# Last gathered rows moved into the last group's second half, gates loaded four keys at once and ahead, sums loaded later

## The chip, the cores and the metric

The kernel runs on one core of one Trainium2 chip. Its engines work beside each other, each through its own list of instructions in order: TensorE (PE, with PEld for its weight loads), VectorE (DVE), ScalarE (ACT), GpSimd (POOL) and SyncE (SP, which here only starts DMA transfers). The metric is the device time of one execution in microseconds (us). A time given for a kernel is the median of several executions; the profile comes from one more execution.

## The reference

One layer: a hybrid mixer, a cross attention over a memory, and a PEER feed-forward layer, each with a residual and a layer norm. The change touches the PEER layer alone. For each of 512 tokens, 8 heads pick 16 of 128 x 128 = 16,384 experts, so 128 experts a token:

```
def block(args):
    xt, it, gt = args
    u = expert_u[it]
    a = jnp.einsum('tkd,td->tk', u, xt, preferred_element_type=F32)
    hact = jax.nn.gelu(a, approximate=False) * gt
    return jnp.einsum('tk,tkd->td', hact.astype(x.dtype), expert_v[it])
...
h = peer_ffn(x, peer_wq[l], peer_sub_keys[l], peer_u[l], peer_v[l])
x = layer_norm(DN_ALPHA * x + h, ln_w[l, 2], ln_b[l, 2])
```

`it` holds the picked experts, `gt` their softmax gates. D is 2048, everything is float32.

## The kernel before, in words

The kernel does the PEER layer in two ways beside each other.

**Gathered half.** Tokens 0 to 255, in two blocks of 128 (`t` = 0 and 1). For each of the 128 picks `k` of a block, `job_u` gathers one row of `peer_u` per token (an indirect DMA of 128 rows of 8 KB, 1 MB, into a `rows` tile, line 1007) and DVE takes its dot product with the token (line 1027). When a block's 128 dots are there, `job_v` gathers rows of `peer_v` and DVE adds them, scaled, to the block's sum `x2l` (line 1043). After the last, `fin_gathered` makes the layer norm of the block and writes it out. `rows` has three buffers; they also serve the norm's weights (`lw`, line 1064) and, once all jobs are handed out and six further weight tiles were loaded, every second weight tile (`load_raw`).

**Dense half.** Tokens 256 to 511 (`H` = 256, two blocks of 128, `HB` = 2) go over all experts. There are `NC_` = 128 keys `c` of 128 experts each. A U tile (1 MB, `next_a`) gives the activations of one key: 48 matmuls into a PSUM bank `pa`, two keys to a bank; then ACT's gelu (line 1288) writes `ga`. 28 of the 64 pairs `ga` are spilled to DRAM (`gad`) and come back later as `gb`. Just ahead of the dense stage the gates are built as a full matrix and written to DRAM (`gd`, eight writes of 2 MB). `stage_h` loads the gates `G` of a pair of keys, multiplies them into `ga`, and splits the product into an upper and a lower part, `hph` and `hpl`. A V tile (1 MB) holds two keys and one half (`dh`) of the 2048 output columns: 24 matmuls into four banks `mm` (lines 1390, 1391 and 1399). Sixteen keys are a group (`J`), and `stage_o` runs a group's eight V tiles of the first column half, then eight of the second; then the banks are added to the sums `acc` (lines 1413 and 1415). 68 keys of U are done ahead of the first group; the rest are mixed into the V tiles by `fill` until they run out. After the last group comes the layer norm of both dense blocks (`fin`).

Each weight tile is split by ACT (upper part, line 179) and DVE (lower part, line 182) into one of two `ring` tiles; float32 is done as three products of such parts. In the dense stage there are three buffers for raw weight tiles.

**What sets the order.** A job is handed out by `tick`, which every split calls: it adds credit (`rate` x cost x `mult`; the rate is the number of jobs over 980 units), and for each whole credit the next gather is given to GpSimd, to start behind that split; its use on DVE is put behind the split two tiles later at the earliest (`lag`). A scheduler with a model of the times then lays each engine's instructions into one fixed order, in which a use can stand later still. The sync engine's list of loads is fixed in the same way; a load whose buffer is not free holds all loads behind it. `after(i, j)` keeps `i` behind `j` in that order without a wait on the chip. `ahead` is the table of how many U tiles are done by which key; `spilled` holds the pairs that go through `gad`.

Of the kernel before, what the change touches and what calls it, by code (L numbers as in the profile page):

```python
# [49 lines left out]
def build(tc, I, out):  # L50
    nc = tc.nc
    NC_ = PKEYS
    with ExitStack() as ctx:
# [981 lines left out]
        def job_v(t, k, s):  # L1035
            rows = gather("peer_v", t, k, s)

            def use(s2):
                d = tok[t]["dots"][k // GB]
                acc = tok[t]["x2l"]  # L1040
                if k == 0:
                    nc.vector.tensor_scalar(acc, acc, ALPHA, None, op0=ALU.mult)
                i = nc.vector.scalar_tensor_tensor(acc, rows, d[:, GB + k % GB:GB + k % GB + 1], acc,  # L1043
                                                   op0=ALU.mult, op1=ALU.add)
                after(i, s2)
                if k == NC_ - 1:
                    fin_gathered(t)
            return use
# [18 lines left out]
        def fin_gathered(t):  # L1067
            acc = tok[t]["x2l"]
            st = gat["pool"].tile([P, 32], F32, tag="fst", bufs=2, name=nm("fst"))
            fin_load()  # L1070
# [237 lines left out]
        def o_bank():  # L1308
            return mm_bank()
# [44 lines left out]
        hs = {}  # L1354
        state["mult"] = 1.0

        def stage_h(c):
            gt = mn.tile([P, H // 64, 2, 64], F32, tag="G", bufs=3, name=nm("G"))
            nc.sync.dma_start(gt, gd[:, :, c:c + 2])
            if c // 2 in spilled:  # L1360
                ga = mn.tile([P, 512], F32, tag="gb", bufs=3, name=nm("gb"))
                nc.sync.dma_start(ga, gad[c // 2])
            else:
                ga = gas.pop(c // 2)
# [8 lines left out]
        def stage_o(c0, dh, fill):  # L1373

            banks = [[o_bank() for g in range(2)] for t in range(HB)]
            for jj in range(J // 2):
                raw = load_raw(I["vD"][c0 // 2 + jj, dh])
                for vh, vl, o, w in shares(raw, 2.0):
                    for j in range(o // 1024, (o + w) // 1024):
# [3 lines left out]
                        if c0 == 0 and dh == 0 and c in (2, 4):  # L1383
                            nc.sync.dma_start(acc[c // 2 - 1], x2d[HB + c // 2 - 1].rearrange("p g c -> p (g c)"))
# [16 lines left out]
            last = c0 + J == NC_  # L1401
            if last and dh == 0:
                if state["done"] < len(jobs):
                    raise RuntimeError(f"{len(jobs) - state['done']} jobs left")
            if last and dh:
                while state["later"]:
                    state["later"].pop(0)[1](state["s"])
                fin_load()
# [24 lines left out]
        while at[0] < ahead[0]:  # L1433
            next_a()
# [88 lines left out]
```

## Time and profile before

| what | value |
|---|---|
| median of 3 runs | 4688.21 us (4683.93 to 4692.0) |
| the profiled execution's own time | 4692.06 us |
| its span | 4690.4 us |
| granted TensorE clock, mean | 0.983 |
| PE busy | 4466.1 us, 95% |
| DVE busy | 3764.6 us, 80% |
| ACT busy | 2233.0 us, 48% |
| POOL busy | 894.8 us, 19% |
| moved by DMA | 1490.81 MB, 318 GB/s over the span |

The page also cuts the span into 40 slices of 117 us; a digit is the busy share of a slice in tenths:

```profile
PE   8999999999999999999999988999989999999985
DVE  7877668557898877888788669799978998888886
PEclk9999999999999999999999999999999999999997
DMA  7899889666788889888799765667999999999995
GB/s 289 323 332 329 319 324 340 231 212 226 281 340 327 324 336 345 333 336 316 261 350 355 263 229 195 237 258 285 373 366 399 405 410 370 385 376 379 390 379 188
```

The dense stage with its V tiles lies in the last ten slices. A "wait" in the trace is time in which an engine stood still and what ended that; the chain of waits is followed back from the last instruction.

### The profile page before, as it was taken

How to read it: one execution, taken by the hardware profiler on the slowest of the kernel's cores; microseconds unless marked ns; L12 is line 12 of the kernel's file. 1: busy time of each engine (PE TensorE's matmuls, PEld its weight loads, DVE VectorE, ACT ScalarE, POOL GpSimd, SP SyncE). 2: the span in 40 equal slices, each digit the busy share in tenths (PEclk: the TensorE clock that was granted, in tenths of full speed). 3: DMA queues.
4: the chain of work that ended last, by engine and by line, in shares of the span. 5: the costliest groups of instructions: out<-in, count | busy, mean ns of one | idle time of the engine just before them, and what ended most of it. 6: DMA issues, size and time to landing. Idle time of an engine off the chain costs nothing. (4 is left out here: it accounts for less than half of the span.)

```text
span 4690.4 us, 65123 instructions
## 1 busy us (share of the span) xinstructions
PE 4466.1 (95%) x25662; PEld 3986.0 (85%) x25662; DVE 3764.6 (80%) x4234; ACT 2233.0 (48%) x3040; POOL 894.8 (19%) x631
## 2 busy tenths in 40 slices
PE   8999999999999999999999988999989999999985
PEld 6888888889888899999899766999988778889984
DVE  7877668557898877888788669799978998888886
ACT  6866766554344323333334674535744333343431
POOL 1000000000222222322221000112122333333430
PEclk9999999999999999999999999999999999999997
DMA  7899889666788889888799765667999999999995
GB/s 289 323 332 329 319 324 340 231 212 226 281 340 327 324 336 345 333 336 316 261 350 355 263 229 195 237 258 285 373 366 399 405 410 370 385 376 379 390 379 188
DMA packets 261204, 1490.81 MB, mean 318 GB/s; under 512 B 27132, under 2 KB 69180, under 8 KB 92320
## 3 DMA queue, kind: packets, MB, share of 16 engines
q1 hardware_dynamic: 167568, 890.57, 50.9%
q0 software_dynamic: 81664, 561.95, 31.0%
q10 hardware_dynamic: 11664, 34.12, 1.8%
q8 instruction: 201, 3.29, 0.3%
q14 instruction: 107, 0.88, 0.1%
HBM read 1427.24 MB, written 59.29 MB: 317 GB/s over the span
## 5 line engine op out<-in xcount | busy, mean ns | idle before, releaser
L179 ACT CAST ring<-raw 128x1024 fp32r<-128x1024 f32 x1568 | 1595.5, 1050 | 1585.5 <-PE mm L201 428.2
L182 DVE TENSOR_TENSOR ring<-raw,ring 128x2048 fp32r<-128x2048 f32 (+1 forms) x926 | 1810.2, 1961 | 574.3 <-ACT ring L179 306.9
L1007 POOL DMA_INDIRECT rows<-in_peer_u,ei x256 | 384.0, 1500 | 1676.6 <-DVE rows L1027 786.3
L201 PE MATMUL mm<-Ah,ring 128*128 128x384 f32 x2560 | 670.4, 342 | 13.4 <-ACT Ah L147 6.2
L1043 DVE SCALAR_TENSOR_TENSOR x2l<-rows,dots,x2l 128x2048 f32<-128x2048 f32 x256 | 601.0, 2348 | 49.5 <-DMA rows<-in_peer_v,ei 48.6
L1007 POOL DMA_INDIRECT rows<-in_peer_v,ei x256 | 443.9, 1734 | 929.3 <-DVE x2l L1043 696.6
L1027 DVE SCALAR_TENSOR_TENSOR rows<-rows,x2l 128x2048 f32<-128x2048 f32 x256 | 582.7, 2284 | 22.0 <-DMA rows<-in_peer_u,ei 21.8
L1277 PE MATMUL pa<-Xh,ring 128*128 128x256 f32 x2048 | 499.8, 285 | 32.3 <-ACT ring L179 16.8
L1280 PE MATMUL pa<-Xl,ring 128*128 128x256 f32 x2048 | 495.6, 282 | 0.0
L201 PEld LDWEIGHTS mm<-Ah,ring 128*128 128x128 f32 x2560 | 463.6, 189 | 20.6 <-ACT Ah L147 7.4
L1390 PE MATMUL mm<-ring,hph 128*128 128x512 f32 x1024 | 405.5, 396 | 63.0 <-ACT ring L179 62.6
L201 PE MATMUL mm<-Al,ring 128*128 128x384 f32 x1280 | 428.9, 341 | 0.6 <-DVE Al L148 0.6
L1277 PEld LDWEIGHTS pa<-Xh,ring 128*128 128x128 f32 x2048 | 389.3, 190 | 39.9 <-ACT ring L179 21.1
L1391 PE MATMUL mm<-ring,hpl 128*128 128x512 f32 x1024 | 403.4, 394 | 0.0
L1280 PEld LDWEIGHTS pa<-Xl,ring 128*128 128x128 f32 x2048 | 389.9, 190 | 2.9
L244 PE MATMUL mm<-ring,Zl 128*128 128x512 f32 x832 | 329.1, 396 | 0.0
L243 PE MATMUL mm<-ring,Zh 128*128 128x512 f32 x832 | 328.3, 395 | 0.7 <-ACT ring L179 0.7
L243 PE MATMUL mm<-ring,Ah 128*128 128x512 f32 x768 | 305.5, 398 | 1.1 <-ACT ring L179 1.1
L244 PE MATMUL mm<-ring,Al 128*128 128x512 f32 x768 | 303.4, 395 | 0.0
L1390 PEld LDWEIGHTS mm<-ring,hph 128*128 128x128 f32 x1024 | 193.9, 189 | 109.0 <-ACT ring L179 67.3
L1284 PE MATMUL pa<-Xh,ring 128*128 128x256 f32 x2048 | 265.7, 282 | 5.3 <-DVE ring L182 5.2
L201 PE MATMUL mm<-Bh,ring 128*128 128x384 f32 x1024 | 262.6, 339 | 5.6 <-ACT ring L179 4.9
(388 smaller groups left out, 7143.2 us busy)
## 6 DMA issues: line engine op xcount, KB each, us to landing
raw<-in_w_in SPq DMA_DIRECT2D x256, 1024.0 KB
raw<-in_uT SPq DMA_DIRECT2D x128, 1024.0 KB
raw<-in_vD SPq DMA_DIRECT2D x128, 1024.0 KB
raw<-in_w_out SPq DMA_DIRECT2D x48, 1024.0 KB
raw<-in_peer_wq SPq DMA_DIRECT2D x48, 1024.0 KB
raw<-in_w_xkv SPq DMA_DIRECT2D x32, 1024.0 KB
raw<-in_w_br_ml SPq DMA_DIRECT2D x32, 1024.0 KB
raw<-in_w_br_fx SPq DMA_DIRECT2D x32, 1024.0 KB
```

The source lines that it names most:

```text
L179: x = nc.scalar.copy(hi[:, c:c + 1024], src[:, c:c + 1024])
L182: s = nc.vector.tensor_sub(lo, src, hi.bitcast(F32))
L201: i = nc.tensor.matmul(o, w, x, start=start and s % per == 0, stop=stop and s % per == per - 1)
L243: nc.tensor.matmul(banks[t], xh[:, tt], wh[:, c], start=k == 0, stop=False)
L244: nc.tensor.matmul(banks[t], xl[:, tt], wh[:, c], start=False, stop=False)
L1007: i = nc.gpsimd.indirect_dma_start(out=rows, out_offset=None, in_=I[table], in_offset=bass.IndirectOffsetOnAxis(ap=ei[t][:, k:k + 1], axis=0))
L1027: i = nc.vector.scalar_tensor_tensor(rows, rows, 1.0, tok[t]["x2l"], op0=ALU.mult, op1=ALU.mult, accum_out=d[:, k % GB:k % GB + 1])
L1043: i = nc.vector.scalar_tensor_tensor(acc, rows, d[:, GB + k % GB:GB + k % GB + 1], acc, op0=ALU.mult, op1=ALU.add)
L1277: i = nc.tensor.matmul(bank, uh[:, sl], xh, start=k == 0, stop=False)
L1280: nc.tensor.matmul(bank, uh[:, sl], xl, start=False, stop=False)
L1390: nc.tensor.matmul(banks[t][g], a[:, tt], vh[:, gs_], start=c == c0, stop=False)
L1391: nc.tensor.matmul(banks[t][g], b[:, tt], vh[:, gs_], start=False, stop=False)
```

## The change

Five things are edited.

- Gates: `ask_g` loads `G` for four keys at once (512 KB, runs of 1024 bytes, two buffers) in place of two keys (256 KB, runs of 512 bytes, three buffers), four keys ahead; the first is asked for three U tiles before the V tiles begin. `ask_a` asks for spilled values four keys ahead. `late` keeps each of these loads behind the latest split in the scheduler's order.
- Sums: the residual is loaded into `acc` at keys 10 and 12 of the first group in place of 2 and 4, and also by `late`.
- `mult`, the factor on the jobs' credit, is 0.925 in place of 1.0 in this stage.
- End of the jobs: all uses must be laid down before the sixth V tile of the last group's second half, in place of the end of its first half (handed out) and its second half (used).
- Norm of the second gathered block: `fin_gathered(1)` is called behind the second last V tile, and shares the norm's weights, loaded once, with the dense blocks.

```diff
--- before.py
+++ after.py
@@ -1043,7 +1043,8 @@
                 i = nc.vector.scalar_tensor_tensor(acc, rows, d[:, GB + k % GB:GB + k % GB + 1], acc,
                                                    op0=ALU.mult, op1=ALU.add)
                 after(i, s2)
-                if k == NC_ - 1:
+                if k == NC_ - 1 and t == 0:
+                    fin_load()
                     fin_gathered(t)
             return use
 
@@ -1067,7 +1068,6 @@
         def fin_gathered(t):
             acc = tok[t]["x2l"]
             st = gat["pool"].tile([P, 32], F32, tag="fst", bufs=2, name=nm("fst"))
-            fin_load()
             for g in range(4):
                 nc.vector.bn_stats(st[:, 6 * g:6 * g + 6], acc[:, g * 512:(g + 1) * 512])
             fin_head(st)
@@ -1351,17 +1351,28 @@
 
         mn = ctx.enter_context(pool("main"))
         acc = [mn.tile([P, D], F32, tag=f"acc{t}", name=f"acc{t}") for t in range(HB)]
-        hs = {}
-        state["mult"] = 1.0
+        hs, g4 = {}, {}
+        state["mult"] = 0.925
+
+        def late(i):
+            after(i, state["s"])
+
+        def ask_g(c):
+            if c < NC_ and c not in g4:
+                g4[c] = mn.tile([P, H // 64, 4, 64], F32, tag="G", bufs=2, name=nm("G"))
+                late(nc.sync.dma_start(g4[c], gd[:, :, c:c + 4]))
+
+        def ask_a(c):
+            if c // 2 in spilled and c // 2 not in gas:
+                gas[c // 2] = mn.tile([P, 512], F32, tag="gb", bufs=3, name=nm("gb"))
+                late(nc.sync.dma_start(gas[c // 2], gad[c // 2]))
 
         def stage_h(c):
-            gt = mn.tile([P, H // 64, 2, 64], F32, tag="G", bufs=3, name=nm("G"))
-            nc.sync.dma_start(gt, gd[:, :, c:c + 2])
-            if c // 2 in spilled:
-                ga = mn.tile([P, 512], F32, tag="gb", bufs=3, name=nm("gb"))
-                nc.sync.dma_start(ga, gad[c // 2])
-            else:
-                ga = gas.pop(c // 2)
+            if c % 4 == 0:
+                ask_g(c + 4)
+            ask_a(c + 4)
+            gt = g4[c - c % 4][:, :, c % 4:c % 4 + 2]
+            ga = gas.pop(c // 2)
             gv = ga.rearrange("p (c b t) -> p c b t", c=2, t=64)
             nc.vector.tensor_mul(gv, gv, gt.rearrange("p b c t -> p c b t"))
             a, b = pair(mn, "hp", J + 2)
@@ -1373,15 +1384,22 @@
         def stage_o(c0, dh, fill):
 
             banks = [[o_bank() for g in range(2)] for t in range(HB)]
+            last = c0 + J == NC_
             for jj in range(J // 2):
+                if last and dh and jj == 5:
+                    if state["done"] < len(jobs):
+                        raise RuntimeError(f"{len(jobs) - state['done']} jobs left")
+                    while state["later"]:
+                        state["later"].pop(0)[1](state["s"])
+                    fin_load()
                 raw = load_raw(I["vD"][c0 // 2 + jj, dh])
                 for vh, vl, o, w in shares(raw, 2.0):
                     for j in range(o // 1024, (o + w) // 1024):
                         c = c0 + 2 * jj + j
                         if dh == 0 and c % 2 == 0:
                             stage_h(c)
-                        if c0 == 0 and dh == 0 and c in (2, 4):
-                            nc.sync.dma_start(acc[c // 2 - 1], x2d[HB + c // 2 - 1].rearrange("p g c -> p (g c)"))
+                        if c0 == 0 and dh == 0 and c in (10, 12):
+                            late(nc.sync.dma_start(acc[c // 2 - 5], x2d[HB + c // 2 - 5].rearrange("p g c -> p (g c)")))
                         a, b = hs[c]
                         for t in range(HB):
                             tt = slice(t * P, (t + 1) * P)
@@ -1398,14 +1416,8 @@
                                 gs_ = slice(j * 1024 - o + g * 512, j * 1024 - o + (g + 1) * 512)
                                 nc.tensor.matmul(banks[t][g], a[:, tt], vl[:, gs_], start=False, stop=c == c0 + J - 1)
                 fill(dh * J + 2 * jj + 1)
-            last = c0 + J == NC_
-            if last and dh == 0:
-                if state["done"] < len(jobs):
-                    raise RuntimeError(f"{len(jobs) - state['done']} jobs left")
-            if last and dh:
-                while state["later"]:
-                    state["later"].pop(0)[1](state["s"])
-                fin_load()
+                if last and dh and jj == J // 2 - 2:
+                    fin_gathered(1)
             for t in range(HB):
                 for g in range(2):
                     o = acc[t][:, dh * 1024 + g * 512:dh * 1024 + (g + 1) * 512]
@@ -1431,6 +1443,13 @@
 
 
         while at[0] < ahead[0]:
+            if at[0] == ahead[0] - 3:
+                ask_g(0)
+            if at[0] == ahead[0] - 2:
+                ask_a(0)
+                ask_a(2)
+            if at[0] == ahead[0] - 1:
+                ask_g(4)
             next_a()
         for c0 in range(0, NC_, J):
             def fill(i, c0=c0):
```

Three places of the engines' lists, as they stand in the built programs. SP at the point where the V tiles draw near; `raw` is a weight tile, `in_uT` and `in_vD` are U and V in DRAM. Before:

```order
L158 DMA raw_28776<-in_uT 128x2048
L1359 DMA G_29138<-gd 128x4x128
L1359 DMA G_29177<-gd 128x4x128
L1384 DMA acc_28656<-x2d 128x2048
L1359 DMA G_29217<-gd 128x4x128
L1384 DMA acc_28657<-x2d 128x2048
L1362 DMA gb_29382<-gad 128x512
L1362 DMA gb_29423<-gad 128x512
L1362 DMA gb_29739<-gad 128x512
L158 DMA raw_28832<-in_uT 128x2048
```

and in the changed kernel:

```order
L158 DMA raw_28776<-in_uT 128x2048
L158 DMA raw_28832<-in_uT 128x2048
L158 DMA raw_28892<-in_uT 128x2048
L158 DMA raw_28950<-in_uT 128x2048
L158 DMA raw_29012<-in_uT 128x2048
L1363 DMA G_28948<-gd 128x4x256
L158 DMA raw_29071<-in_uT 128x2048
L158 DMA raw_29134<-in_vD 128x2048
L1363 DMA G_29069<-gd 128x4x256
```

Eight loads of gates, sums and spilled values stood between two U tiles; now four U tiles come first, then one gate load of four keys.

DVE near the end of the program, before. These are the last rows of a run of 11 uses of gathered rows that stand in one block behind the split of `raw_37012`, then the gathered block's norm, then the split of a V tile:

```order
L1043 SCALAR_TENSOR_TENSOR x2l_22788<-rows_36553,dots_30812,x2l_22788 128x2048
L1043 SCALAR_TENSOR_TENSOR x2l_22788<-rows_36593,dots_30812,x2l_22788 128x2048
L1072 BN_STATS fst_36686<-x2l_22788 128x6 x4
L1051 BN_AGGR fst_36686<-fst_36686 128x2
L267 TENSOR_SCALAR fst_36686<-fst_36686 128x1
L1055 SCALAR_TENSOR_TENSOR x2l_22788<-x2l_22788,fst_36686,lw_36687 128x1024 x2
```

and in the changed kernel, around its last four V tiles:

```order
L182 TENSOR_TENSOR ring_19878<-raw_37125,ring_19878 128x2048
L182 TENSOR_TENSOR ring_105<-raw_37160,ring_105 128x2048
L1043 SCALAR_TENSOR_TENSOR x2l_22788<-rows_37067,dots_30918,x2l_22788 128x2048
L182 TENSOR_TENSOR ring_19878<-raw_37189,ring_19878 128x2048
L1043 SCALAR_TENSOR_TENSOR x2l_22788<-rows_37099,dots_30918,x2l_22788 128x2048
L1072 BN_STATS fst_37218<-x2l_22788 128x6 x4
L1052 BN_AGGR fst_37218<-fst_37218 128x2
L267 TENSOR_SCALAR fst_37218<-fst_37218 128x1
L1056 SCALAR_TENSOR_TENSOR x2l_22788<-x2l_22788,fst_37218,lw_37156 128x1024 x2
L182 TENSOR_TENSOR ring_105<-raw_37237,ring_105 128x2048
```

The block of uses is gone; the last ones stand singly between splits, and the norm's first half stands between the splits of the last two V tiles, where before it stood ten V tiles from the end.

SP at the end of the program, before. `raw_36976` and `raw_37048` are V tiles in `rows` buffers:

```order
L158 DMA raw_37012<-in_vD 128x2048
L158 DMA raw_37098<-in_vD 128x2048
L158 DMA raw_37156<-in_vD 128x2048
L158 DMA raw_37214<-in_vD 128x2048
L1064 DMA lw_36687<-in_ln_w 128x2048
L1064 DMA lw_36689<-in_ln_b 128x2048
L158 DMA raw_36976<-in_vD 128x2048
L158 DMA raw_37048<-in_vD 128x2048
```

and in the changed kernel:

```order
L158 DMA raw_37125<-in_vD 128x2048
L158 DMA raw_37160<-in_vD 128x2048
L158 DMA raw_37189<-in_vD 128x2048
L1065 DMA lw_37156<-in_ln_w 128x2048
L158 DMA raw_37237<-in_vD 128x2048
L1065 DMA lw_37158<-in_ln_b 128x2048
L1077 DMA out<-x2l_22788 128x1024 x2
```

Before, V tile `raw_36976` is multiplied ahead of `raw_37012` (by its number) but its load stands behind both norm weights; now only the last V tile stands behind one of them.

## The prediction

> **What bounds the kernel now.** I read the page's slices first, then the windows of the last stage, then the chain of waits in the one window where TensorE (PE) stands still. The stage from 3480 us on (the dense second half of the PEER layer, with the gathered first half beside it) is cut here at its own boundaries. Columns: span, busy time (and instructions) of PE, weight load, DVE, ACT and POOL, granted clock, DMA share, GB/s.
>
> ```profile
> 3480.00:3560.00 80.00, 61.91 (x436) 59.22 (x435) 57.54 (x50) 30.67 (x38) 14.13 (x11) 0.87 1.03 401
> 3560.00:3880.00 320.00, 312.40 (x1334) 249.55 (x1332) 292.70 (x250) 123.27 (x141) 95.56 (x56) 0.99 1.01 404
> 3880.00:4552.00 672.00, 661.98 (x4266) 603.19 (x4267) 590.23 (x331) 270.06 (x299) 253.00 (x118) 1.00 0.97 379
> 4552.00:4608.20 56.20, 9.20 (x56) 7.90 (x54) 44.09 (x33) 5.80 (x8) 14.68 (x11) 0.61 0.90 352
> 4608.20:4670.30 62.10, 62.09 (x262) 50.39 (x263) 28.38 (x19) 19.63 (x19) 0.00 (x0) 0.97 0.39 146
> 4670.30:4690.40 20.10, 0.68 (x3) 0.20 (x2) 15.80 (x30) 0.41 (x2) 0.00 (x0) 0.57 0.26 104
> ```
>
> PE is the bound nearly everywhere: its idle time is 18.1 us at the start (80.00 − 61.91), 7.6 us while only V tiles run, 10.0 us while U and V tiles alternate, 47.0 us in the fourth row, none in the fifth. The last row is the final norm, 20.1 us, with PE done. The DMA queues are as full as PE: share 0.97 to 1.03 up to 4552, then 0.39 after 4608. So the kernel has one big hole at the end, and empty DMA time only behind it.
>
> The chain of waits through the hole, in order of time (start, length, what):
>
> ```profile
> 4556.87 10.87 DMA rows<-in_peer_v,ei
> ...
> 4570.45 8.15 DMA rows<-in_peer_v,ei
> ...
> 4581.32 7.29 DMA rows<-in_peer_v,ei
> ...
> 4591.32 6.38 DMA rows<-in_peer_v,ei
> 4597.79 2.36 DVE x2l L1043
> 4600.17 6.92 DMA raw<-in_vD
> 4607.11 1.05 ACT ring L179
> 4608.21 0.79 PE mm L1390
> ...
> 4619.29 1.81 PE mm L1399 x8
> 4624.83 1.87 PE mm L1399 x8
> ```
>
> ```profile
> PE mm L1390 <- ACT ring L179: 47.0, 1, 47.0
> ```
>
> PE does not lack arithmetic: it waits for one V tile. That tile was given a `rows` buffer, and the buffer is free only when the last gathered row has been used (4597.79 + 2.36 = 4600.15); its load starts at 4600.17. Ahead of that, 11 gathers are drained one behind another. In the order of the vector engine the gathers have fallen behind their tickets: counted in weight tiles, a use stands 9 to 10 tiles behind its job's own tile in the middle of the stage and 18 to 19 near the end. The first V tile after the hole takes about 7.4 us (4608.21 to the end of its last products near 4615.6) instead of 5.54 (4624.83 − 4619.29), under a granted clock that was down to 0.61 (fourth row).
>
> **The change, part by part.**
>
> *1. The last gathers (multiplier 0.925, drain at the sixth tile of the last half, no V tile in a `rows` buffer).* In the new order the lag falls to 3 tiles by the middle and stays there. All V tiles use their own three raw buffers, since the jobs never run out more than 6 tiles before the end. So nothing ties a V tile to a gather, and the 47.0 us wait goes, with it about 1.2 us of slow clock: 11 V tiles run from 4608.2 to 4670.3, 62.1 us, against 11 × 5.54 = 60.9.
>
> What is late next? The 11 gathers now lie beside the last 12 V tiles. Three resources have to carry this.
>
> ```profile
> L182 DVE TENSOR_TENSOR ring<-raw,ring 128x2048 fp32r<-128x2048 f32 x199 | 452.5, 2288 | 87.2 <-ACT ring L179 57.3 <-PE mm L1399 22.2 <-issue 4.3
> L1043 DVE SCALAR_TENSOR_TENSOR x2l<-rows,dots,x2l 128x2048 f32<-128x2048 f32 x128 | 300.6, 2349 | 36.4 <-DMA rows<-in_peer_v,ei 35.6
> 4600.17 2.47 DVE L1072 BATCH_NORM_STATS2 fst<-x2l 128x6 f32<-128x512 f32 x4
> 4603.05 2.47 DVE L1055 SCALAR_TENSOR_TENSOR x2l<-x2l,fst,lw 128x1024 f32<-128x1024 f32 x2
> ```
>
> DVE: 2.29 + 2.35 = 4.64 us a tile, under 5.54. DMA: two loads of 1.05 MB in 5.54 us are 379 GB/s, which is what the row 3880 to 4552 moved while PE was 98.5% busy, and less than the 404 of the row above it. The new wait is the norm of the last gathered token block, which DVE now does between the splits of the last two V tiles. Behind the split of the second last tile stand one use (2.35), the statistics (2.47), two small ones (0.4) and the first half of the norm (2.47): 7.7 us, queued ahead of the last tile's split. With two ring tiles, a split may start when PE has done the tile two before it, at T. The second last split ends at T + 2.3, the last one starts at T + 10.0 and ends at T + 12.3. PE needs it after one whole tile and the 16 products with the upper part, T + 5.5 + 5.5 + 3.7 (two thirds of a tile) = T + 14.7. So 2.4 us of slack: cost nothing, and if the last gather lands later, each us beyond 2.4 is a us at the end. The SP queue: the load of ln_w stands ahead of the last V tile's load and waits for the third last gather's use, which by then is done. One pair of norm-weight loads falls away (2.1 MB, before in the row with share 0.39: worth nothing). The second half of the norm (0.8 us of small steps and 2.5 us) lies beside that tile's products.
>
> I charge the 11 tiles with the pace of the V-only row, where one gather per tile runs beside other loads. The same windows for line 1390 alone (8 per V tile):
>
> ```profile
> 3560.00:3880.00 320.00, 175.43 (x443) 83.33 (x442) 0.99 1.01 404
> ```
>
> 443 / 8 = 55.4 tiles in 320 us, 5.78 us each, so 11 × (5.78 − 5.54) = 2.7 us. **Term: −47.0 − 1.2 + 2.7 = −45.5 us** (bounds −48.2, and −17 if each gather took its full 2.6 us, 1.05 MB at 404 GB/s, from PE: 11 × 2.6 = 28.6 in place of 2.7, −19.6, and up to 2.6 more for the norm).
>
> *2. The start: U tiles ahead of the gates, sums' loads later.* The SP queue before, and what PE waited for from 3480 to 3560:
>
> ```profile
> 3480.03 1.27 SPq L1359 DMA_DIRECT2D G<-gd  x2
> 3481.35 8.92 SPq L1384 DMA_DIRECT2D acc<-x2d  x1
> 3490.31 2.24 SPq L1359 DMA_DIRECT2D G<-gd  x1
> 3492.60 1.44 SPq L1384 DMA_DIRECT2D acc<-x2d  x1
> 3494.14 1.88 SPq L1362 DMA_DIRECT2D gb<-gad  x3
> 3498.02 0.33 SPq L158 DMA_DIRECT2D raw<-in_uT  x1
> ...
> PE pa L1277 <- ACT ga L1288: 15.4, 2, 9.0
> ...
> 3458.63 0.82 ACTq L1347 DMA_DIRECT2D gd<-stage  x2
> ...
> gd<-stage ACTq DMA_DIRECT2D x8, 2048.0 KB
> ```
>
> The queue serves gates, sums and spilled values for 18 us, while the next U tile, which PE needs first, stands behind them. ACT is in order too: its two gelus that free PE's bank stand behind casts of `hph` that need a gate. In the new order four U tiles go first, then one gate load, and the gelus stand ahead of the `hph` casts. Some of this wait stays (the two writes of 2 MB to `gd`, issued at 3458.63, still fill the queues). But bytes only move: acc's 2.1 MB and the early gates go into the V-only stretch, whose DMA share is 1.01. So PE can gain here only what the queues gain.
>
> *3. Four keys per gate load.* The same bytes in half the packets (1024 B runs in place of 512 B). No row times such a packet; I bound it from the window 3560 to 3880 (packets, MB, share of 16 engines; then issues):
>
> ```profile
> q1 hardware_dynamic: 24529, 71.22, 56.3%
> q0 software_dynamic: 7938, 57.82, 44.0%
> ...
> raw<-in_vD SPq DMA_DIRECT2D x53, 1024.0 KB
> G<-gd SPq DMA_DIRECT2D x25, 256.0 KB
> gb<-gad SPq DMA_DIRECT2D x22, 256.0 KB
> raw<-in_uT SPq DMA_DIRECT2D x2, 1024.0 KB
> ```
>
> q0 (the gathers): 0.440 × 320 × 16 / 7938 = 0.284 us for 7.28 KB, 25.7 KB per us. q1: 0.563 × 5120 = 2883 engine-us. The 55 raw tiles (7040 packets of 8 KB, 0.319 each) take 2247, gb (2816 of 2 KB, 0.080) 225, which leaves 411 for 12,800 gate packets, 0.032 us against 0.020 at the bulk rate. A 1 KB packet then costs between 0.040 (all of the surplus goes) and 0.052 (none of it per packet): 0.19 to 0.39 us of all 16 engines saved for each old load. The 37 old loads up to 3880 give 7 to 14 us, the 27 behind them 5 to 11. From the gain I take off some 2 us for the gathers that the smaller lag brings forward. **Terms: −10 us up to 3880** (bounds 0 and the idle 18.1 + 7.6 = 25.7), **−2 us from 3880 to 4552** (bounds 0 and the idle 10.0; PE is 98.5% busy there, so I take it near zero).
>
> The Trainium skill, *DMA: Bandwidth & Descriptors*, section Specifications, puts the least transfer for line rate at 512 B; by that the old gate packets are already at line rate and nothing is saved. The 0.032 against 0.020 above speaks against it, but as a remainder of large numbers. By the rule the sum would be the first rival's.
>
> **Sum.** −45.5 − 10 − 2 = −57.5. The profiled execution took 4692.06 us (span 4690.4): 4634.6. The median of the three runs lies 3.85 us lower, 4688.21, and the new time is a median too: **4631 us**. The final 20.1 us stay: same instructions behind the last product, the table load for the square root now comes with the earlier norm and not in this tail.
>
> **Rivals.**
>
> *Queues give nothing (0.22).* The gates cost the same bytes per us, and the start's gain is given back in the V-only stretch, whose share of 1.01 has no room. Only part 1 is left: 4688.2 − 45.5 = 4643. For it: share 1.03 at the start, 1.01 behind. Against it: the remainder above, and SP standing 18 us ahead of a needed tile.
>
> *All the idle time goes (0.10).* The waits are the order's and not the queues': −48.2 − 25.7 − 10.0 = −83.9, 4604. For it: the named waits are for in-order queues. Against it: the 4 MB of gates still written at the start.
>
> *The gathers slow the last tiles (0.08).* V tiles have three buffers there instead of six, and each gather takes its DMA time from PE: −19.6 in place of −45.5, 4657. It decides if the queues move less than 379 GB/s there.
>
> *Slower (0.05).* With a lag of 3 tiles and three row buffers, a gather has some 3 × 5.54 = 16.6 us from issue to use; its landing took 6.4 to 10.9 us above. Should it exceed 16.6, each use holds DVE, which is in order, so the splits and PE behind it. Now uses wait 24.4 us in all:
>
> ```profile
> DVE x2l L1043 <- DMA rows<-in_peer_v,ei: 24.4, 15, 4.3
> ```
>
> That is 0.2 us for each of 115. To pass 4698 it must eat 67 us in some 145 uses, 0.46 us each on PE's path. Since buffers, not tickets, set the issue before, I see no reason for it.
>
> *Nothing moves (0.02).* The hole would reappear at the last tile, behind the norm, at 4688; but in the program's order no more than three gathers can be outstanding there.
>
> **Chances.** The forecast has 0.53, with its own range 4620 to 4640. Range for 8 in 10: from 4610, part of the way to 4604, to 4655, past 4643, just short of 4657. A change under 0.2% (9 us) can't be told from none. Faster by more: 0.53 + 0.22 + 0.10 + 0.08 = 0.93; within: 0.02; slower: 0.05.
>
> **What would show it.** Right: no wait of PE over 10 us behind 4500, the gather uses going on until some 20 us before PE's last product, DMA share near 0.9 in the last 60 us before it instead of 0.39; SP issuing U tiles between 3480 and 3498; packets down by some 16,000. Wrong: a PE wait on the last V tile's split longer than 2 us (the norm's slack), PE's pace above 5.8 us a tile in the last 12 (queues), or V tiles from 3560 to 3880 slower than 5.78 us (the start's gain given back).

## The result, and the profile after

| | median | runs | ratio to before, 95% interval |
|---|---|---|---|
| before, same series | 4692.0 us | 5 (4683.93 to 4700.88) | |
| changed | 4664.56 us | 5 (4654.5 to 4677.99) | 0.9945 [0.9927, 0.9963] |

The change gains 27 us, 0.55%; forecast were 57, and the time lies above the range. The windows of the last stage, cut as for before (span, busy time and instructions of PE, weight load, DVE, ACT, POOL, granted clock, DMA share, GB/s):

```profile
3480.00:3560.00 80.00, 68.24 (x504) 65.39 (x503) 60.45 (x46) 31.94 (x37) 23.60 (x12) 0.94 1.00 402
3560.00:3880.00 320.00, 292.35 (x1193) 231.18 (x1192) 272.55 (x234) 114.22 (x129) 87.42 (x53) 0.95 0.97 384
3880.00:4552.00 672.00, 663.04 (x4197) 600.17 (x4196) 586.51 (x337) 268.30 (x296) 251.94 (x117) 0.99 0.95 379
4552.00:4608.00 56.00, 53.53 (x303) 46.75 (x302) 52.08 (x32) 24.16 (x28) 24.60 (x10) 0.97 1.01 411
4608.00:4656.00 48.00, 48.00 (x210) 38.95 (x209) 44.05 (x37) 15.78 (x16) 12.91 (x4) 1.00 0.68 264
4656.00:4676.30 20.30, 1.30 (x6) 0.73 (x4) 16.05 (x31) 0.41 (x2) 0.00 (x0) 0.63 0.38 153
```

The big hole is gone: row four, with 47.0 us of idle PE before, has 2.5. The start is better (11.8 us idle instead of 18.1). But the V-only row (3560 to 3880, where only V tiles are multiplied), which had 7.6 us of idle PE, now has 27.65, and its granted clock fell from 0.99 to 0.95. What PE waits for, over the whole execution (us in total, times, longest):

```profile
PE mm L1408 <- ACT hph L147: 22.4, 9, 4.7
...
PE pa L1277 <- ACT ga L1288: 11.0, 2, 10.2
...
PE mm L1409 <- DVE hpl L148: 6.7, 4, 2.6
```

The first and the last row are new. `hph` and `hpl` are the two halves of the gated hidden rows, which V tiles are multiplied with; before, PE waited for neither in this stage. And the V products (line 1408, 8 per tile), 3560 to 3880:

```profile
3560.00:3880.00 320.00, 156.32 (x398) 77.81 (x397) 0.95 0.97 384
```

398 / 8 = 49.8 tiles, 6.43 us each, where before took 5.78.

Profiled executions differ by up to 14 us in what lies ahead of the change: the last product of the gate build (line 1340) starts at 3456.3 before and at 3464.9 in the changed kernel. So I compare the stage from there to the end, cut at the first V product and the last U product. All runs are in this table; "V-only" counts PE's products in the 320 us from the first V product. Each run's ratio is to runs of before on its own chip.

| run | gate build to first V | to last U | to the end | stage | V-only | median us | ratio, 95% |
|---|---|---|---|---|---|---|---|
| before | 94.0 | 1005.2 | 134.9 | 1234.1 | 1329 | 4692.0 | |
| changed | 83.1 | 1038.4 | 89.9 | 1211.4 | 1204 | 4664.6 | 0.9945 [0.9927, 0.9963] |
| e1 | 91.2 | 1004.2 | 94.9 | 1190.3 | 1330 | 4647.8 | 0.9905 [0.9890, 0.9920] |
| e2 | 82.2 | 1050.8 | 126.6 | 1259.6 | 1207 | 4714.0 | 1.0051 [1.0038, 1.0065] |
| e3 | 82.5 | 1020.1 | 93.3 | 1195.9 | 1289 | 4654.3 | 0.9922 [0.9908, 0.9936] |
| e4 | 85.7 | 1011.7 | 94.9 | 1192.3 | 1294 | 4647.1 | 0.9902 [0.9887, 0.9917] |
| e5 | 85.3 | 1013.0 | 94.9 | 1193.2 | 1294 | 4654.2 | 0.9916 [0.9902, 0.9929] |
| e6 | 81.1 | 1046.5 | 98.8 | 1226.4 | 1274 | 4679.2 | 0.9968 [0.9956, 0.9980] |
| e7 | 83.5 | 1029.2 | 95.4 | 1208.1 | 1279 | 4667.3 | 0.9949 [0.9935, 0.9962] |
| e8 | 86.3 | 1011.3 | 96.0 | 1193.6 | 1295 | 4654.1 | 0.9920 [0.9907, 0.9934] |
| e9 | 84.5 | 1082.2 | 104.8 | 1271.5 | 1179 | 4729.4 | 1.0073 [1.0060, 1.0087] |
| e10 | 83.7 | 1042.2 | 100.6 | 1226.5 | 1206 | 4684.5 | 0.9978 [0.9969, 0.9987] |
| e11 | 97.9 | 1024.2 | 95.0 | 1217.1 | 1255 | 4677.5 | 0.9965 [0.9951, 0.9978] |

The change's stage: start −10.9, middle +33.2, end −45.0, in sum −22.7. The middle is the riddle. Of its 33 us, 30 are lost in the V-only stretch (125 products fewer at 320 / 1329 = 0.241 us each).

One such loss in the changed kernel, in order of time on ACT, DVE and PE (start, length, engine, operation; in brackets how long the engine stood idle and what ended it):

```profile
3647.33 1.04 ACT L179 CAST ring<-raw 128x1024 fp32r<-128x1024 f32 x1
3657.98 1.22 ACT L147 CAST hph<-gb 128x512 fp32r<-128x512 f32 x2 [9.60 <-DVE gb L1377]
3659.10 1.99 ACT L179 CAST ring<-raw 128x1024 fp32r<-128x1024 f32 x2
```

```profile
3648.42 2.29 DVE L1027 SCALAR_TENSOR_TENSOR rows<-rows,x2l 128x2048 f32<-128x2048 f32 x1
...
3650.63 2.29 DVE L1027 SCALAR_TENSOR_TENSOR rows<-rows,x2l 128x2048 f32<-128x2048 f32 x1
...
3652.84 2.29 DVE L182 TENSOR_TENSOR ring<-raw,ring 128x2048 fp32r<-128x2048 f32 x1
3655.05 2.28 DVE L1027 SCALAR_TENSOR_TENSOR rows<-rows,x2l 128x2048 f32<-128x2048 f32 x1
...
3657.26 1.29 DVE L1377 TENSOR_TENSOR gb<-gb,G 128x512 f32<-128x512 f32 x2
...
3661.12 2.29 DVE L182 TENSOR_TENSOR ring<-raw,ring 128x2048 fp32r<-128x2048 f32 x1 [1.20 <-ACT ring L179]
```

```profile
3652.04 2.03 PE L1417 MATMUL mm<-ring,hph 128*128 128x512 f32 x8
3658.65 2.07 PE L1408 MATMUL mm<-ring,hph 128*128 128x512 f32 x4 [4.58 <-ACT hph L147]
...
3663.08 0.63 PE L1408 MATMUL mm<-ring,hph 128*128 128x512 f32 x1
3663.51 0.63 PE L1409 MATMUL mm<-ring,hpl 128*128 128x512 f32 x1
...
3664.76 0.39 PE L1408 MATMUL mm<-ring,hph 128*128 128x512 f32 x1
3664.99 0.39 PE L1409 MATMUL mm<-ring,hpl 128*128 128x512 f32 x1
```

ACT is in order. Its next instruction is the cast of `hph`, which needs the gate product (line 1377) of DVE. DVE is not idle: it works through three dot products of gathered rows (line 1027) and a weight split (line 182) that stand ahead of the product. The product itself waits for nothing but its place: nowhere in this stage does DVE of the changed kernel stand for a gate or a spilled value. ACT stands 9.60 us, and behind the cast stands the next weight tile's cast, so DVE's next split is late too; PE stands 4.58 us, and for some 6 us behind that its products start 0.43 us apart (3663.08, 3663.51) in place of 0.23 (3664.76, 3664.99).

Where does that place come from? `late` lays each gate and spill load behind the latest weight split in the scheduler's order. By its own reckoning the gate then comes later, and it lays the product that needs the gate later on DVE. Counted in DVE's order, before's split of `hpl` stands mostly 7 weight splits ahead of the split of its own V tile; in the changed kernel's V-only stretch six of eight pairs in a group (five in the first group) stand −2 to 0 ahead, that is level with it or behind.

### The profile page after: what moved, and what is told of

Read it like the earlier page. It is cut to its first block, busy times and chain, and to the rows that moved or that the text cites. A ratio compares the mean times of both kernels' runs of the same rounds, so it can differ in the third digit from the quotient of the medians.

```text
span 4676.3 us, 65083 instructions
## 1 busy us (share of the span) xinstructions
PE 4487.3 (96%) x25662; PEld 4002.2 (86%) x25662; DVE 3763.9 (80%) x4234; ACT 2236.3 (48%) x3040; POOL 918.3 (20%) x631
## 4 chain that ended last, share of the span: by engine, by line
PE 64%; DVE 6%; DMA 4%; ACT 3%; issue 2%; ACTq 0%; POOL 0%; DVEq 0%; SPq 0%; POOLq 0%
PE mm L201 20%; PE mm L243 5%; PE mm L251 5%; PE mm L244 5%; PE mm L1409 4%; PE pa L1284 4%; PE mm L1408 4%; PE pa L1277 4%; PE pa L1280 4%; PE mm L1417 4%; DVE ring L182 2%; DMA gad<-ga 1%; DMA rows<-in_peer_v,ei 1%; ACT ring L179 1%; PE mm L1340 1%
## 5 line engine op out<-in xcount | busy, mean ns | idle before, releaser
L1007 POOL DMA_INDIRECT rows<-in_peer_v,ei x256 | 462.5, 1807 | 939.4 <-DVE x2l L1043 681.7
L1027 DVE SCALAR_TENSOR_TENSOR rows<-rows,x2l 128x2048 f32<-128x2048 f32 x256 | 583.2, 2285 | 21.7 <-DMA rows<-in_peer_u,ei 21.7
```

Source lines behind the costliest of these rows:

```text
L1007: i = nc.gpsimd.indirect_dma_start(out=rows, out_offset=None, in_=I[table], in_offset=bass.IndirectOffsetOnAxis(ap=ei[t][:, k:k + 1], axis=0))
L1027: i = nc.vector.scalar_tensor_tensor(rows, rows, 1.0, tok[t]["x2l"], op0=ALU.mult, op1=ALU.mult, accum_out=d[:, k % GB:k % GB + 1])
```

## Experiments

The theories as the expectations name them. **L** (lead): the ties move the gate product and the halves of `h` too late in DVE's and ACT's order. **C** (crowding): the paced gathers put more work on gathered rows onto DVE in the V-only stretch. **Q** (queues): what the start gains, the full DMA queues take back there. The expectations count 1333 (before) and 1209 (changed) products in the V-only stretch; these are sums over four windows of 80 us, in which a product on a boundary counts twice. One window of 320 us gives 1329 and 1204.

**e1, the end alone.** The changed kernel's multiplier, drain and norm; gates and sums as before.

```diff
-        state["mult"] = 1.0
+        state["mult"] = 0.925
...
+                if last and dh and jj == 5:
...
+                    while state["later"]:
+                        state["later"].pop(0)[1](state["s"])
+                    fin_load()
...
+                if last and dh and jj == J // 2 - 2:
+                    fin_gathered(1)
```

> The change's end and job rate with the gates, spilled values and sums loaded as before. Theory L (lead: the gates' products are laid down too late because each gate load is tied to the latest split): nothing of the loss is here, the hole of 47 us is gone, ratio 0.988 to 0.992 (about -45 us), V tiles alone idle under 10 us from the first V tile to the first U tile between them. Theory C (crowding: the gathers' uses, brought forward by the smaller lag, hold DVE): the loss stays, ratio 0.994 to 0.996, PE waits for hph or hpl over 15 us.

**e2, gates and sums alone.** The changed kernel with `state["mult"] = 1.0` and before's drain and norm.

> The change's gates, spilled values and sums with the end, rate and drain of before. Theory L: the loss is all here: 20 us or more of PE waits for hph and hpl, the start's 10 us gained, the hole of 40 to 50 us stays; ratio 1.000 to 1.006. Theory C: no such waits, only the start's gain; ratio 0.997 to 0.999.

Their windows of the V-only stretch, e1 then e2:

```profile
3552.80:3872.80 320.00, 311.66 (x1330) 249.40 (x1331) 293.38 (x248) 127.44 (x145) 97.29 (x55) 0.99 1.01 406
```

```profile
3545.10:3865.10 320.00, 293.22 (x1207) 232.26 (x1207) 274.34 (x236) 116.66 (x133) 92.42 (x53) 0.95 0.97 385
```

The loss comes with the gates and not with the end: e1 gains 43.5 us (4691.4 for before in this series), e2 loses 22.7, with a hole of 38.9 us left at its end. C falls: e2 loses as much in the V-only stretch with before's multiplier, and e1, with the changed one, loses nothing. The parts nearly add up: the stage gives −43.8 + 25.5 = −18.3 for the two, −22.7 for the whole.

**e3, the ties only up to the first V tile's split**, which all later loads are laid behind:

```diff
         def late(i):
-            after(i, state["s"])
+            after(i, top[0] if top else state["s"])
...
         def stage_h(c):
+            if not top:
+                top.append(state["s"])
```

> The whole change, but from the first V tile on the gate and spill loads are kept behind one fixed split (the latest when V begins) and no longer behind the latest at each time. The uses of the gates then stand 7 or more splits ahead of their V tile. Theory L: start gained (10 us), hole gone (45 us), no PE waits for hph over 5 us: ratio 0.986 to 0.990, about 4635 us. Theory Q (queues: what the start puts off has to be moved while V tiles run, so V tiles lose it whatever the order): as the changed kernel, 0.994 to 0.996, with 20 us or more of PE idle while V tiles run alone, now waiting for raw V tiles.

**e4, no ties on gates and spilled values** (the four-key loads, asked for four keys ahead, and the end stay):

```diff
-                late(nc.sync.dma_start(g4[c], gd[:, :, c:c + 4]))
+                nc.sync.dma_start(g4[c], gd[:, :, c:c + 4])
...
-                late(nc.sync.dma_start(gas[c // 2], gad[c // 2]))
+                nc.sync.dma_start(gas[c // 2], gad[c // 2])
```

> The whole change with the gate and spill loads tied to no split at all; they go ahead of the U tiles again. Theory L: the V tiles lose nothing, the start loses its gain, the hole is gone: ratio 0.988 to 0.992, the start's PE idle in the 80 us behind the last write of the gates back to about 18 us. Theory C: loss stays, 0.994 to 0.996.

With the ties gone e4 gains 44.3 us; its `hpl` stands mostly 7 to 8 splits ahead again, PE waits for neither half, and the V-only stretch has 1294 products. That is still 35 fewer than before. e4's ratio came as L had it, but by luck in the parts: the start kept most of its gain, which was expected to go, and the V tiles lost some 8 us, which were expected to lose nothing. e3 fell between the two ranges of its expectation (0.9922). In its first group `hpl` still stands 0 to 4 splits ahead and only then 7 or more; PE waits for neither half, and the stretch has 1289 products, though the start is the second best of the four:

```profile
3537.90:3857.90 320.00, 306.46 (x1289) 242.67 (x1288) 290.33 (x253) 122.73 (x143) 86.64 (x53) 0.98 1.01 407
```

The DMA share there is 1.01, as before. e4's start is 8.3 us shorter than before's, and 6.5 come back up to the last U tile; e3's is 11.5 shorter, and 14.9 come back. So Q fits what becomes of the start's gain, and e1, which leaves the gates alone, is as fast as e4. But no run isolates the queues. In e4 idle PE grew there by 4.7 us (11.9 against 7.2), and one wait of 3.4 us is for the first group's sum on DVE (line 1425; 0.3 before), whose second part stands there behind a weight split and two dot products. That is a matter of order, not of a transfer.

**e5, the packets.** As e4 with two keys a load (buffers of two keys, four of them, asked for six keys ahead).

```diff
-                g4[c] = mn.tile([P, H // 64, 4, 64], F32, tag="G", bufs=2, name=nm("G"))
+                g4[c] = mn.tile([P, H // 64, 2, 64], F32, tag="G", bufs=4, name=nm("G"))
...
-            if c % 4 == 0:
-                ask_g(c + 4)
+            ask_g(c + 6)
```

> As e4_no_late (four keys a gate load, no tie), but with two keys a load again, in four buffers of the same size together and asked six keys ahead, so that the lead of the gate products stays as in e4_no_late while the gate packets double: 32 loads of 8,192 packets of 512 B in place of 16 loads of 1 KB packets. The third term of the prediction (each of the small loads costs 78 to 155 engine-us, 14 to 16 loads more in this stage, over 16 engines and partly hidden) expects 7 to 14 us more than e4_no_late's 4647.1, that is 4654 to 4661, ratio 0.992 to 0.9935. The theory that the packets are worth next to nothing (in e4_no_late 7,691 packets fewer saved 1.3% of 16 engines over 320 us, some 4 us of the queues, and its time was that of e1_end_only) expects 4645 to 4651, ratio 0.990 to 0.9915.

(Two slips in that text: a two-key load has 512 packets, and the 78 to 155 engine-us are those of 25 loads together.) The load queue's row (packets, MB, share of 16 engines) in the V-only stretch, e4 then e5:

```profile
q1 hardware_dynamic: 18206, 71.37, 55.4%
```

```profile
q1 hardware_dynamic: 25174, 72.07, 57.4%
```

6968 more packets and 0.70 MB more took 2.0% of 5120 engine-us, 102. At the gathers' bulk rate of 25.7 KB per us the bytes are 27 of these, so a packet costs (102 − 27) / 6968 = 0.011 engine-us. Before against e4 gives (56.7 − 55.4)% of 5120 for 7691 packets, 0.009. The prediction had 0.012 to 0.024. Over 320 us that is some 4 to 5 us of all queues. Whether any reaches the time stays open: the stage says 0.9 us, the intervals of the ratios (0.9916 against 0.9902) overlap, and e5's ratio lies between the two ranges of its expectation.

**e6 and e7, the dose.** The changed kernel with its ties laid behind the split two back (e6) or four back (e7); e7's edit:

```diff
             state["s"] = s
+            state.setdefault("past", []).append(s)
...
-            after(i, state["s"])
+            after(i, state["past"][-5])
```

> The changed kernel with its gate and spill loads tied not to the latest split but to the one two splits before it; nothing else. By the order of DVE the split of the gated hidden rows then stands 0 to 1 weight splits ahead of its V tile in the V-only stretch, where the changed kernel has -2 to 0. Theory L (the time went where the gate product stands too late for its V tile) expects about half of the loss back: 1240 to 1290 matmuls in the first 320 us of V (changed kernel 1209, before 1333), V tiles to the last U tile 1015 to 1030 us (changed kernel 1038), ratio 0.991 to 0.9935. Rival: the tie itself costs, because the loads come from their queue later or collide there with the weight tiles; two splits more change that little: 1200 to 1225 matmuls, 1033 to 1042 us, ratio 0.994 to 0.996.

> As e6_tie_two_back with the tie four splits back: the split of the gated hidden rows then stands 2 to 3 weight splits ahead of its V tile in the V-only stretch. Theory L expects nearly all of the loss back, and the start's gain kept as far as the queues let it: 1280 to 1320 matmuls in the first 320 us of V, V tiles to the last U tile 1005 to 1018 us, ratio 0.989 to 0.991. Rival (the tie itself costs): still 1200 to 1240 matmuls, 1030 us or more, ratio 0.993 to 0.996.

The V-only stretches are about as L has them (1274, and 1279 where 1280 was the least), and PE waits for `hph` and `hpl` in neither. But the ratios missed L's ranges: e7's lies in the rival's, e6's is worse than both. The loss moved. e6 lost 30 of its 35 us against e4 behind that stretch, where U and V tiles alternate, and the new wait there is for the weight splits:

```profile
PE mm L1409 <- ACT ring L179: 16.6, 9, 3.6
PE pa L1278 <- ACT ring L179: 12.0, 3, 6.5
```

Ahead of the longest one, on ACT and on DVE of e6:

```profile
4386.91 0.62 ACT L147 CAST hph<-ga 128x512 fp32r<-128x512 f32 x1 [9.67 <-DVE ga L1378]
4387.43 1.99 ACT L179 CAST ring<-raw 128x1024 fp32r<-128x1024 f32 x2
```

```profile
4383.92 2.35 DVE L1043 SCALAR_TENSOR_TENSOR x2l<-rows,dots,x2l 128x2048 f32<-128x2048 f32 x1 [5.06 <-DMA rows<-in_peer_v,ei]
4386.19 1.28 DVE L1378 TENSOR_TENSOR ga<-ga,G 128x512 f32<-128x512 f32 x2
```

The product stands behind a gather sum whose rows have not landed. DVE stands 5.06 us for the gather, ACT 9.67 for the product, and the weight tile behind the cast comes 6.5 us late to PE, though by DVE's order the tile that needs the cast's own result is still 3 or more splits away. So here a count of splits ahead is not what decides; it is whether ACT meets the cast before the product is through DVE, with a needed weight tile queued behind. Two things are left open: whether e6's shorter waits come about in the same way, and why the changed kernel lost less there. The changed kernel's ACT stood for products in the mixed stretch even longer than e6's, while PE lost little by it there.

**e9, the product late, no load late.** After e6 and e7 a rival was alive: the tied loads themselves cost. e9 is e4 with the tie on the product:

```diff
-            nc.vector.tensor_mul(gv, gv, gt.rearrange("p b c t -> p c b t"))
+            after(nc.vector.tensor_mul(gv, gv, gt.rearrange("p b c t -> p c b t")), state["s"])
```

> As e4_no_late (no load tied, so the gate loads stand on SP's queue as early as there), but with the gate product itself tied on DVE behind the latest weight split. By the order of DVE each product then stands one weight split behind that of its own V tile, in all eight pairs of a group, where the changed kernel has six of eight so in the V-only stretch and 1 to 3 ahead in the mixed one. Theory L in the form that the runs of the ties two and four back left it (the price is the place of the product on DVE behind gather sums, and ACT, which stands in order before it with the weight splits behind) expects the loss without any late load: ACT waits 80 us or more for the product in the first 320 us of V (changed kernel 55, before 20), at most 1220 matmuls there (e4_no_late 1294, changed kernel 1204), V tiles to the last U tile 1038 us or more (e4_no_late 1011.7), ratio 0.9945 to 1.004. Rival (the tied loads cost, by their place on SP's queue or by landing late): as e4_no_late, 1280 to 1300 matmuls, 1008 to 1016 us, ratio 0.989 to 0.9915.

```profile
3547.40:3867.40 320.00, 288.32 (x1179) 227.59 (x1180) 270.73 (x235) 117.09 (x132) 82.92 (x51) 0.94 0.96 377
```

```profile
PE mm L1409 <- DVE hpl L148: 15.3, 7, 4.2
PE mm L1408 <- ACT hph L147: 13.3, 6, 5.3
```

With no load tied, the place of the product alone costs 70 us between the first V and the last U tile (1082.2 against 1011.7) and makes the kernel slower than before, and slower than L's range (1.0073, where 1.004 was the most). In DVE's order `hpl` stands −2 to −1 splits ahead in every pair, and DVE never stands for a gate or a spilled value. ACT's wait for the product was less than expected (52 us, not 80): here PE waits for the halves directly. So the loss needs no late load. For the rival nothing speaks in the changed kernel's trace either: DVE never stands for a tied load there, and ACT waits 39 us for raw V tiles in the V-only stretch, where before waits 76. That the ties cost nothing at all beside the product's place is not shown.

**e10 and e11, the product on GpSimd**, in the changed kernel and in e1:

```diff
-            nc.vector.tensor_mul(gv, gv, gt.rearrange("p b c t -> p c b t"))
+            nc.gpsimd.tensor_mul(gv, gv, gt.rearrange("p b c t -> p c b t"))
```

> The changed kernel, ties and all, with its gate product on GpSimd in place of DVE. There it stands behind gather issues in place of gather sums. Theory L expects that ACT no longer waits for DVE's product; if GpSimd has it done in time (its product takes some 1 to 3 us where DVE's takes 0.69, an estimate from the ratio of nothing measured here, so the wait may move to GpSimd), 1260 to 1310 matmuls in the first 320 us of V, V tiles to the last U tile 1005 to 1025 us, ratio 0.989 to 0.992; if the product then waits on GpSimd behind an issue that waits for its buffer, ACT waits for GpSimd as long as it did for DVE and the time is the changed kernel's or more. Rival (the tied loads themselves cost): no wait for a product, yet 1200 to 1230 matmuls and 1035 us or more, ratio 0.994 to 0.996.

> e1_end_only with its gate product on GpSimd. There the products stand 7 or more weight splits ahead and TensorE never waits for them, so theory L expects no gain from the product's place: at most the 44 us of DVE that 64 products of 0.69 us leave free (DVE is 90% busy in the V-only stretch, and TensorE waits 8 us in 320 there), 4636 to 4650, ratio 0.9880 to 0.9915. The rival, that products on GpSimd hold up the gathers' issues, would show as waits of DVE for gathered rows and a time above 4655.

What ACT of e10 waits for, and GpSimd's queue, in the V-only stretch:

```profile
ACT hph L147 <- POOL gb L1377: 85.8, 15, 10.1
```

```profile
POOL rows L1007 <- DVE rows L1027: 185.9, 40, 12.3
```

On GpSimd the product takes 1.3 to 2.6 us, mostly (0.69 on DVE), and stands behind gather issues that wait 186 of 320 us for DVE to free their buffers. So the wait moved with it (85.8 us, 55 in the changed kernel); this is the expectation's second branch. e11 puts the product there in a kernel in which PE had no such wait, and is 30 us slower than e1. Its own expectation of a gain missed. The time is the rival's, but not its sign: in the V-only stretch DVE waits for gathered rows 3.6 us (1.9 in e1), while ACT's wait for the product grew from 20.5 to 46.3 us and PE's for weight splits from 9.7 to 20.8. The freed DVE time bought nothing.

**e8, the end's last 5 us.** From the last U tile to the end the changed kernel takes 89.9 us and e1 and e4 94.9, because there the last gathered block's norm comes behind the last product. e8 is e4, paced by 0.88 and then 0.955, with the last split laid behind that norm:

```diff
+                    if last and dh and jj == J // 2 - 1:
+                        after(state["s"], normed)
```

> As e4_no_late, with two edits at the end: the tickets of the gathers paced by 0.88 in the first three groups and 0.955 after (a gather's sum then lies 3 to 5 weight splits behind its ticket in the last group, where e4_no_late has 5 to 7), and the last V tile's split on DVE ordered behind the norm of the last gathered block, which in e4_no_late slips behind the last product. From the last U tile to the end e4_no_late takes 94.9 us and the changed kernel, whose norm stands ahead of that split, 89.9. If the norm behind the last product is what those 5 us are, 89 to 91 us and 4640 to 4644, ratio 0.9885 to 0.9900; if the last split, held behind the norm and the last sums, makes TensorE wait as long, 94 to 98 us and 4646 to 4651, ratio 0.990 to 0.9915.

```profile
4624.95 3.78 PE L1420 MATMUL mm<-ring,hph 128*128 128x512 f32 x8 [7.17 <-DVE ring L182]
```

```profile
4613.99 2.47 DVE L1072 BATCH_NORM_STATS2 fst<-x2l 128x6 f32<-128x512 f32 x4
...
4622.61 2.28 DVE L182 TENSOR_TENSOR ring<-raw,ring 128x2048 fp32r<-128x2048 f32 x1
```

PE waits 7.17 us for that split: 96.0 us, no gain, and at 4654 us the time lies above both expectations. But e8 does not copy the changed kernel's order. There one gathered sum and the first half of the norm stand between the last two weight splits; in e8 two sums and the whole norm stand there. The last split ends 12.2 us behind the start of the second last in the changed kernel, 19.2 in e8. Of the 7 us, 3.4 are the norm's second half (4619.26 to 4622.61), the rest the second sum and a wait of 1.32 us for its rows. So a norm that is forced ahead costs here what it saves; e8 with the first half alone was not run.

e1 and e4 beat both kernels; they differ from each other by less than can be told.

## Why the prediction was wrong

*Term 1, the end, was right in its mechanism:* −45.5 forecast, −45.0 measured (134.9 to 89.9). The hole went, DMA share is 1.01 and 0.68 where it was 0.90 and 0.39, and the norm cost nothing, as the slack of 2.4 us had it. That the sum is so close is luck in its small parts. The last tiles did not pay the 2.7 us for a slower pace (210 products in 48.0 us are 5.5 us a tile), and the 1.2 us of slow clock did not come back: without the holes the 288 products behind the last U tile take 68.4 us, before 68.5. In their place stands one wait of 2.5 us for `hph`, which the prediction does not have. The table load for the square root was not in before's tail either (the last stands at 4560.5); nothing hangs on it.

*Term 2, the start, was right in itself:* the gate build reaches the first V tile 10.9 us earlier, SP issues U tiles first, and the two gelus' wait went from 15.4 to 11.0 us; some of it stayed, as expected.

*Term 3 was too large,* with 0.009 to 0.011 engine-us a packet instead of 0.012 to 0.024. By the Trainium skill, *DMA: Bandwidth & Descriptors*, Specifications, 512 B are enough for line rate. The packets of e4 and e5 speak for a small cost all the same, too small to be seen in the time.

*The step that failed:* "−10 us up to 3880", and its bounds 0 and the idle 25.7. Up to there the change cost, it did not gain: −10.9 + 30.1 = +19. Some of the 30 fits the rival "queues give nothing" (0.22): e4, without ties, is 35 products short, 8.4 us, and gives back most of its start; that the queues are the reason is argued, not shown. The larger part, the 90 products between e4 and the changed kernel, 21.7 us, no case held. The prediction followed the moved loads on SP's queue and through the DMA windows, and gave `late` no price of its own. What an order laid on a load does to the instruction that consumes it, and to the two in-order engines that this and the cast stand on, is missing from it, though DVE's order shows it: `hpl` 7 splits ahead before, −2 to 0 after. The bound "0" was no bound. The sign that the prediction named, V tiles slower than 5.78 us, came (6.43), but most of it has this other cause. The rival "slower" had half of the mechanism, a held DVE with splits and PE behind it, but only for gathers that land late.

*The mixed stretch,* −2 forecast, came to +3.

Without the ties the time comes near the first rival's (45.5 off, 4643): e1 and e4 came 43.5 and 44.3 off, at 4648 and 4647. Here too the parts differ: their ends save 40.0 and not 45.0, since the gathered block's norm comes behind the last product in both, and their starts save 2.8 and 8.3.

## What to carry to other kernels

Where a scheduler orders instructions, a dependency that is laid on a load moves its consumers too: before pricing such an edit, compare where the consumer stands on its compute engine, and what stands behind it there. In these runs a hand-over between two in-order engines (DVE's product, ACT's cast) cost most when the waiting instruction stood ahead of work that the bound engine needed next; it belongs several tiles ahead, not at the tile. And where the DMA queues are full in the next stretch, a gain from moving loads into it may only be lent: e4 gave back 6.5 of 8.3 us, e3 more than it had gained.

## What the runs showed of the hardware

Holes on PE of 4 to 5 us cost more than their length. The V-only stretch, before and then changed:

```profile
3550.30:3870.30 320.00, 312.84 (x1329) 250.15 (x1330) 292.86 (x248) 127.81 (x145) 95.84 (x55) 0.99 1.01 405
```

```profile
3548.00:3868.00 320.00, 292.35 (x1204) 231.34 (x1203) 273.85 (x235) 115.09 (x130) 90.74 (x53) 0.95 0.97 383
```

Idle PE grew by 312.84 − 292.35 = 20.5 us, but 30.1 us of products were lost; the other 9.6 are slower products. The granted clock in the 6.4 us behind the hole shown above is 0.52:

```profile
3658.60:3665.00 6.40, 6.35 (x16) 4.99 (x17) 5.17 (x4) 3.54 (x4) 0.16 (x1) 0.52 1.01 425
```

The sum of the holes does not decide this. e6 has 20.2 us of idle PE in the same stretch, in holes of at most 3.2 us, and a granted clock of 0.99; e11 has less, 18.6 us, with one hole of 4.1 us, and 0.97. e6's row:

```profile
3543.50:3863.50 320.00, 299.83 (x1274) 237.81 (x1273) 282.55 (x243) 122.04 (x141) 94.70 (x53) 0.99 1.00 399
```

In the changed kernel the longest is 4.7 us, at 0.95, and in e9 5.3 us, at 0.94. Over all thirteen traces the stretch has 0.94 to 0.97 where the longest hole is 4.1 us or more, and 0.97 to 0.99 where it is 3.4 us or less. The Trainium skill, *TensorE: Matmul & The Clock Gate*, section "HAM oscillation — how this bites in real kernels", has the rule that PE must not idle longer than about 3.4 us. These runs agree, but they do not show where between 3.2 and 4.1 us the limit lies.
